# Opening of a decoder-layer kernel: memory keys' projection with all low parts on Vector, loads in halves, the identity loaded by itself, and the second memory block transposed behind the first products

## The chip, the cores and the metric

One core of a Trainium2 chip. The time is device microseconds of one launch, the median of three runs. A profile is taken of one further execution; its rows give microseconds from the start of the span.

## The reference

One inference step of one decoder layer, for a prompt of 512 rows and a sample group of 8 x 4 rows, width 1024: a mixer (mLSTM heads beside differential attention), cross-attention into 256 memory tokens, and a gated MLP with a causal convolution. The change lies in how the kernel opens: with the memory keys of the cross-attention.

```python
def mem_kv(mem, g_mem_src, w_mk, w_mv):
    B = mem.shape[0]
    mn = rms_norm(mem, g_mem_src)
    mk = (mn @ w_mk).reshape(B, MEM_TOKENS, MEM_HEADS, MEM_HEAD_DIM)
    mv = (mn @ w_mv).reshape(B, MEM_TOKENS, MEM_HEADS, MEM_HEAD_DIM)
    return mk, mv

def rms_norm(x, g):
    xf = x.astype(jnp.float32)
    y = xf * lax.rsqrt(jnp.mean(xf * xf, axis=-1, keepdims=True) + RMS_EPS)
    return (y * g.astype(jnp.float32)).astype(x.dtype)

# layer(): the mixer's input is projected next, and memory keys are used later
    h = rms_norm(x, g_mix_pre)
    z = h @ w_in
```

`mem` is 256 x 1024 and `w_mk` 1024 x 1024, all in float32; `mk` is also an output.

## The kernel before, in words

**Products in three.** Each float32 operand is split into a high part, cast to a rounded 32-bit format on ScalarE (`nc.scalar.copy`), and a low part, the difference, on Vector (`tensor_tensor` with SUB). A product a x b is high x high + high x low + low x high: three matmuls (L411, L412 and L413 in `gemmA`; L472 and L485 in `gemmB`). `split` writes both parts; `put` does it for activations and can give the low part to another engine, and `split_w` does it for weights.

**Memory keys.** `mem_k` computes two halves of 512 columns each. A half takes 8 steps of k (128 rows of the weights each) for two blocks of 128 memory rows: 2 x 8 x 2 x 3 = 96 matmuls of 128x128 by 128x512. A weight tile (`slotA`) holds two steps of k, 256 x 512 float32, 512 KB; eight of them, in a ring of 4 slots of split tiles behind 6 staging buffers. `W.get` takes the next tile, `W.free` gives a slot back, and `W.pump` then issues the next tile's load and split. With `share=True` a tile is cast whole on ScalarE (L221); Vector and GpSimd then compute one half of its low part each (L223).

**Memory rows.** `mem_in(b)` loads a block (`xms`, 512 KB). `norm_turn` transposes it on TensorE against the identity (L332, eight 128x128 transposes in two groups of four), multiplies by the gain on Vector (L334, out `ht`), and splits it by `put` into `memT` (L146 the high part, L147 the low part); with `pool=(True, False)` the first group's low part is GpSimd's, the second's Vector's. The root mean square isn't applied to the rows but to the result: `mrs` (sum of squares on ScalarE, L309; power on GpSimd, L304; copy on Vector, L540) scales the accumulator in `ev` (L548). The scaled result is stored and transposed for the cross-attention.

**The opening.** Block 0's rows, the constants `cpk` (identity, rotary tables and small selectors, 199 KB) and one row of gains are loaded. Nine warm-up matmuls run (`NWARM`), the gains are transposed (L177), block 0 is turned, seven fill matmuls follow (`NFILL`), and block 1 is turned. `W.nslots` is 1, then 2, then 4 between the loads, which sets in which order weight tiles and rows are asked for.

**The x blocks.** While `mem_k` runs, the prompt's rows (four blocks of 128, and 32 sample rows) are normalised and turned into `hT` at the steps of `mem_k` named by `HSTEPS`. A step is a yield of `gemmA`: steps 0 to 7 are the first half's k, 8 its end, 9 to 16 the second half's k, 17 its end. Behind `mem_k` the next projection (`gemmB`, L472) reads `hT`; it works through the first 256 columns of `hT` (two blocks) before it needs the others.

**Order.** Each engine and each DMA queue (SP's and ScalarE's) works in order. The order is made by a scheduler from the program's order as priority and its own idea of times; `tc.issue_after(ins)` puts what is traced in it behind `ins` on that engine, and `tc.high_priority()` (in `burst`) ahead of the rest.

## Time and profile before

| | |
|---|---|
| median of 3 runs | 939.5 us (939.25 to 940.07) |
| the profiled execution | 939.88 us, span 938.1 us |
| TensorE (PE) busy | 914.0 us, 97% of the span, 6778 matmuls |
| Vector (DVE) busy | 607.4 us, 65% |
| ScalarE (ACT) busy | 377.8 us, 40% |
| GpSimd (POOL) busy | 223.7 us, 24% |
| DMA | 130.59 MB, mean 139 GB/s |
| mean granted TensorE clock | 0.996 |

A row of a timeline gives start, duration, engine, line, operation, output<-inputs, shape and count; in brackets at its end stands the engine's idle time before it and what ended that. "ACTq" and "SPq" rows are DMA issues on the queues of ScalarE and SP. A row with xN covers N instructions one after the other. TensorE is busy in nearly all of the span, so what matters is where it isn't.

### The profile page before, as it was taken

The page shows a single profiled execution, that of the slowest core. Times are in us where ns is not written, and L with a number is a line of the kernel's source. Part 1 is how long each engine was busy: PE and PEld are TensorE (multiplying, and loading weights), DVE is VectorE, ACT ScalarE, POOL GpSimd, SP SyncE. Part 2 cuts the span into 40 slices and gives each one's busy share as a digit, 9 for nine tenths or more (in the row PEclk, how much of TensorE's full clock was granted, in tenths as well). Part 3 has the DMA queues.
Part 4 walks back from the last instruction along what each step waited for, and adds up shares of the span by engine and source line. Part 5 has one row for each costly group of instructions (what it writes and reads, how often), then busy time and mean ns, then how long its engine had stood idle before and what let it go on. Part 6 is the DMA issues. An engine that isn't in the chain of part 4 may idle for free.

```text
span 938.1 us, 17455 instructions
## 1 busy us (share of the span) xinstructions
PE 914.0 (97%) x6778; PEld 798.0 (85%) x6778; DVE 607.4 (65%) x1130; ACT 377.8 (40%) x728; POOL 223.7 (24%) x474
## 2 busy tenths in 40 slices
PE   7999999999999999999999999999999999999994
PEld 5899787879866778998777899889988998999974
DVE  5845144565887438686645778637757775776767
ACT  5745233344586447724434533322212222222232
POOL 6611000034442116570000553001100110110114
PEclk9999999999999999999999999999999999999998
DMA  8950023334780339967956632062054304413023
GB/s 286 311 180 11 1 90 138 90 103 161 243 296 8 136 117 298 310 201 243 312 189 172 198 115 69 26 180 69 27 135 135 92 5 120 128 48 90 24 94 117
DMA packets 120834, 130.59 MB, mean 139 GB/s; under 512 B 8599, under 2 KB 86264, under 8 KB 120752
## 3 DMA queue, kind: packets, MB, share of 16 engines
q1 hardware_dynamic: 114568, 125.96, 42.8%
q10 hardware_dynamic: 6184, 3.53, 1.3%
q8 instruction: 53, 0.87, 0.4%
q14 instruction: 29, 0.24, 0.1%
HBM read 112.54 MB, written 16.93 MB: 138 GB/s over the span
## 4 chain that ended last, share of the span: by engine, by line
PE 79%; DVE 8%; DMA 5%; ACT 3%; issue 3%; POOL 2%; SPq 0%; DVEq 0%; ACTq 0%; POOLq 0%
PE mm L485 31%; PE mm L411 6%; PE mm L412 6%; PE mm L413 6%; PE mm L472 4%; PE mm L1837 3%; PE mm L1841 3%; PE mm L1840 3%; PE sda L1256 2%; DVE xb L1165 2%; DMA wst<-in_cache_mem_k_dram 1%; PE mm L390 1%; PE cpo L1480 1%; DVE wslot L147 1%; PE oda L1284 1%
## 5 line engine op out<-in xcount | busy, mean ns | idle before, releaser
L485 PE MATMUL mm<-fT,wslot 128*128 128x256 f32 x1872 | 235.9, 288 | 0.0
L485 PEld LDWEIGHTS mm<-fT,wslot 128*128 128x128 f32 x1872 | 234.3, 188 | 1.8 <-issue 0.8
L146 ACT CAST wslot<-wst 128x1024 fp32r<-128x1024 f32 x125 | 130.7, 1050 | 261.0 <-issue 72.5
L147 DVE TENSOR_TENSOR wslot<-wst,wslot 128x1024 fp32r<-128x1024 f32 x125 | 154.3, 1238 | 81.7 <-ACT wslot L146 81.1
L1837 PE MATMUL mm<-wslot,act 128*128 128x512 f32 (+1 forms) x180 | 69.3, 387 | 0.0
L1840 PE MATMUL mm<-wslot,act 128*128 128x512 f32 (+1 forms) x172 | 67.0, 391 | 0.0
L1841 PE MATMUL mm<-wslot,act 128*128 128x512 f32 (+1 forms) x172 | 66.8, 392 | 0.0
L1739 POOL COPY cvo<-u 128x2 f32<-128x2 f32 x43 | 10.4, 243 | 217.1 <-DVE u L1737 217.1
L411 PE MATMUL mm<-wslot,hT 128*128 128x512 f32 x128 | 51.3, 402 | 0.0
L413 PE MATMUL mm<-wslot,hT 128*128 128x512 f32 x128 | 51.0, 399 | 0.0
L485 PE MATMUL mm<-hT,wslot 128*128 128x256 f32 (+1 forms) x384 | 50.9, 289 | 0.0
L412 PE MATMUL mm<-wslot,hT 128*128 128x512 f32 x128 | 50.8, 397 | 0.0
L1734 DVE TENSOR_TENSOR u<-mm,rsb 128x256 f32<-128x256 f32 x43 | 18.1, 423 | 48.9 <-PE mm L485 48.8
L485 PEld LDWEIGHTS mm<-hT,wslot 128*128 128x128 f32 x384 | 49.2, 188 | 0.5 <-issue 0.2
L1837 PEld LDWEIGHTS mm<-wslot,act 128*128 128x128 f32 x180 | 34.3, 191 | 8.0 <-issue 0.4
L1841 PEld LDWEIGHTS mm<-wslot,act 128*128 128x128 f32 x172 | 32.3, 188 | 6.9 <-issue 0.4
L1840 PEld LDWEIGHTS mm<-wslot,act 128*128 128x128 f32 x172 | 32.3, 188 | 6.9
L1751 ACT ACTIVATE c<-c 128x560 f32<-128x560 f32 x21 | 14.1, 672 | 56.8 <-DVE c L1745 56.7
L1745 DVE SCALAR_TENSOR_TENSOR c<-u,cvT,c 128x560 f32<-128x560 f32 x43 | 34.3, 798 | 0.9
L1744 DVE SCALAR_TENSOR_TENSOR c<-u,cvT,c 128x560 f32<-128x560 f32 x43 | 34.1, 793 | 0.2
L1852 DVE TENSOR_TENSOR yp<-mm,yp 128x512 f32<-128x512 f32 (+1 forms) x41 | 27.1, 672 | 5.1 <-PE mm L1841 5.1
L413 PEld LDWEIGHTS mm<-wslot,hT 128*128 128x128 f32 x128 | 24.1, 188 | 5.0
(493 smaller groups left out, 1858.0 us busy)
## 6 DMA issues: line engine op xcount, KB each, us to landing
wst<-in_w_up_dram SPq DMA_DIRECT2D x42, 512.0 KB
wst<-in_w_in_dram SPq DMA_DIRECT2D x28, 512.0 KB
wst<-in_w_down_dram SPq DMA_DIRECT2D x20, 512.0 KB
kvt<-in_cache_mem_k_dram SPq DMA_DIRECT2D x10, 512.0 KB
kvt<-in_cache_mem_v_dram SPq DMA_DIRECT2D x10, 512.0 KB
wst<-in_w_mk_dram SPq DMA_DIRECT2D x8, 512.0 KB
xb<-in_x_prompt_dram SPq DMA_DIRECT2D x8, 512.0 KB
wst<-in_cache_dk_dram SPq DMA_DIRECT2D x16, 256.0 KB
```

The source lines that it names most:

```text
L146: nc.scalar.copy(out=hi, in_=src)
L147: (eng or nc.vector).tensor_tensor(out=lo, in0=src, in1=f32(hi), op=SUB)
L411: mm(ps[b], lhsT=xt.hi(k, c0, c0 + n), rhs=s[:, 0, kk, :], start=(k == 0), stop=False)
L412: mm(ps[b], lhsT=xt.hi(k, c0, c0 + n), rhs=s[:, 1, kk, :], start=False, stop=False)
L413: return mm(ps[b], lhsT=xt.lo(k, c0, c0 + n), rhs=s[:, 0, kk, :], start=False, stop=(k == nk - 1))
L472: done[0] = mm(ps, lhsT=s[:, l, k, :], rhs=x(k, c0, c1), start=(k == 0 and l == 0 and x == xt.hi), stop=(k == 7 and x == xt.lo))
L485: mm(ps[i], lhsT=s[:, l, k, :], rhs=x(k, c0, c1), start=(k == 0 and j == 0), stop=(k == 7 and j == 2))
L1744: STT(out=c, in0=u[:, 1:EXT - 1], scalar=w[1], in1=c, op0=MUL, op1=ADD)
L1745: STT(out=c, in0=u[:, 0:EXT - 2], scalar=w[0], in1=c, op0=MUL, op1=ADD)
L1837: mm(ps, lhsT=t[:, 0, c0:c0 + P], rhs=s[:, 0, i % 2, cs], start=st, stop=False)
L1840: mm(ps, lhsT=t[:, 0, c0:c0 + P], rhs=s[:, 1, i % 2, cs], start=False, stop=False)
L1841: return mm(ps, lhsT=t[:, 1, c0:c0 + P], rhs=s[:, 0, i % 2, cs], start=False, stop=en)
```

## The change

- The identity has a tile of its own (64 KB), loaded first on ScalarE's queue; the gain row follows it there, off SP's queue. The other constants are loaded on SP's queue behind the second weight tile.
- The memory rows are loaded in two halves of 512 columns. The first two weight tiles of the first half of `mem_k` are loaded, cast and split in two halves each (one step of k each).
- All low parts of the memory keys' weights, of `memT` and of `hT` are on Vector.
- `gemmA` has `first`: products of block 1 at k = 0 and 1 are held; block 1 is turned behind block 0's first three products, and the held ones follow. Products of k > 1 are issued behind the transposes last traced at that point.
- `HSTEPS` goes from (1, 4, 7, 10, 13) to (5, 7, 9, 11, 13); the second x block is loaded at step 1, the other gains are transposed at step 5, and the sums of squares of the memory rows are made at step 3 with their copies on GpSimd.

```diff
-    HORD, HSTEPS = [0, 1, 2, 3, 4], (1, 4, 7, 10, 13)
+    HORD, HSTEPS = [0, 1, 2, 3, 4], (5, 7, 9, 11, 13)
...
-    cpk = cst.tile([P, MASK0], F32, name="cpk")
+    ident = cst.tile([P, P], F32, name="ident")
+    cpk = cst.tile([P, MASK0 - P], F32, name="cpk")
...
     def mem_in(b):
-        dma(out=xms[b], in_=I["mem_prompt"][0, b * P:(b + 1) * P, :])
+        for c in (slice(0, 512), slice(512, DM)):
+            dma(out=xms[b][:, c], in_=I["mem_prompt"][0, b * P:(b + 1) * P, c])
 
     mem_in(0)
-    nc.scalar.dma_start(out=cpk, in_=I["consts"][:, :MASK0])
-    grow = gains_in(0, 1, nc.sync)
+    nc.scalar.dma_start(out=ident, in_=I["consts"][:, :P])
+    grow = gains_in(0, 1, nc.scalar)
...
     def split_w(sv, st, share):
 
-        if share != True:
-            split(sv[:, 0], sv[:, 1], st, share or None)
+        if share:
+            for k in range(2):
+                split(sv[:, 0, k], sv[:, 1, k], st[:, k])
             return
-        m = st.shape[1] // 2
-        nc.scalar.copy(out=sv[:, 0], in_=st)
-        for e, c in ((nc.vector, slice(0, m)), (nc.gpsimd, slice(m, 2 * m))):
-            e.tensor_tensor(out=sv[:, 1, c], in0=st[:, c], in1=f32(sv[:, 0, c]), op=SUB)
+        split(sv[:, 0], sv[:, 1], st)
...
             if nrow == 256:
-                dma(out=st, in_=w[r0:r0 + 256, n0:n0 + 512].rearrange("(k p) n -> p k n", p=P))
+                for k in range(2) if share else ():
+                    dma(out=st[:, k], in_=w[r0 + k * P:r0 + k * P + P, n0:n0 + 512])
+                if not share:
+                    dma(out=st, in_=w[r0:r0 + 256, n0:n0 + 512].rearrange("(k p) n -> p k n", p=P))
                 split_w(sv, st, share)
...
     def norm_T(x, n, gname, xt, c0):
-        norm_turn(norm_rows(x, n), n, gname, xt, c0)
+        norm_turn(norm_rows(x, n), n, gname, xt, c0, (False, False))
...
                 for b in blocks:
-                    if b < 4:
-                        t = one(b, k, s)
+                    if first and b and k < 2:
+                        held.append((b, k, s))
+                    elif b < 4:
+                        with tc.issue_after(turned[0].ins) if first and k > 1 else nullcontext():
+                            t = one(b, k, s)
+                if first and k == 0:
+                    ahead = t.ins
+                if first and k == 1:
+                    with tc.issue_after(ahead):
+                        first()
+                    for x in held:
+                        t = one(*x)
...
     for n0 in (0, 512):
-        slotsA(w_mk, n0, True)
+        for k in range(0, 8, 2):
+            slotA(w_mk, k, n0, share=(n0 == 0 and k < 4))
...
     mem_in(1)
     W.nslots = 2
     W.pump()
+    dma(out=cpk, in_=I["consts"][:, P:MASK0])
     kept = []
-    for b in range(2):
-        kept.append(norm_turn(xms[b], P, "g_mem_src", memT, b * P))
-        if b == 0:
-
-            t = turned[0].ins
-            fill = mmp("fill")
-            for _ in range(NFILL):
-                with burst(t):
-                    t = mm(fill, lhsT=warm[:, 0:P], rhs=warm, start=True, stop=True).ins
-    for b in range(2):
-        VCP(out=mrs[:, b:b + 1], in_=rstd(sumsq(xms[b], P, N("hN")), P, 1, DM))
+
+    def turn(b):
+        kept.append(norm_turn(xms[b], P, "g_mem_src", memT, b * P, (False, False)))
+
+    turn(0)
+    t = turned[0].ins
+    fill = mmp("fill")
+    for _ in range(NFILL):
+        with burst(t):
+            t = mm(fill, lhsT=warm[:, 0:P], rhs=warm, start=True, stop=True).ins
...
-            yield from gemmA(memT, 8, [0, 1], ev)
+            yield from gemmA(memT, 8, [0, 1], ev, first=None if i else lambda: turn(1))
...
-    gains(1, 5, gains_in(1, 5, GQ))
-    VTS(out=gT[:, 36:40], in0=gT[:, 36:40], scalar1=1.0 - LAM_INIT, scalar2=None, op0=MUL)
-    h_in(HB[1])
+    grow = gains_in(1, 5, GQ)
     for i, _ in enumerate(mem_k()):
+        if i == 1:
+            h_in(HB[1])
+        if i == HSTEPS[0]:
+            gains(1, 5, grow)
+            VTS(out=gT[:, 36:40], in0=gT[:, 36:40], scalar1=1.0 - LAM_INIT, scalar2=None, op0=MUL)
+        if i == 3:
+            for b in range(2):
+                nc.gpsimd.tensor_copy(out=mrs[:, b:b + 1], in_=rstd(sumsq(xms[b], P, N("hN")), P, 1, DM))
         if i in HSTEPS:
             j = HSTEPS.index(i)
             norm_T(xbs[HB[j]], rows(HB[j])[1], "g_mix_pre", hT, rows(HB[j])[0])
```

## The prediction

> **What bounds the kernel now.** I read the page first, then busy time in stretches, then the TensorE timeline of the first 40 us, the chain of waits, and the other engines' and the DMA issuing queues' timelines for the same stretch.

> ```profile
> span 938.1 us, 17455 instructions
> ```
> ```profile
> 0.00:15.00 15.00, 10.29 (x43) 5.46 (x44) 6.44 (x13) 9.00 (x14) 8.47 (x18) 1.00 0.90 291
> 15.00:66.00 51.00, 51.00 (x342) 46.79 (x343) 33.62 (x45) 30.37 (x51) 26.42 (x31) 1.00 0.83 256
> 66.00:340.00 274.00, 270.85 (x1968) 221.60 (x1967) 152.72 (x368) 127.98 (x298) 56.63 (x76) 1.00 0.36 116
> ```
> After the stretch's length these rows give busy time of PE, PEld, DVE, ACT and POOL, then granted clock, DMA share and GB/s. TensorE has no hole from 15 to 66 us and 3.15 us of them in the 274 us behind. What the change touches can therefore only pay before 15 us, and pays in full only if nothing runs dry between 15 and 66 us.

> ```profile
> 5.59 0.19 PE L177 MATMUL gps<-cpk,grow 8*128 8x8 f32 x1 [0.34 <-DMA grow<-in_g_mem_src_dram]
> 5.71 1.09 PE L332 MATMUL tp<-cpk,xm 128*128 128x128 f32 x8
> 6.64 1.67 PE L538 MATMUL fill<-warm 128*128 128x512 bf16 x7
> 9.08 0.50 PE L411 MATMUL mm<-wslot,memT 128*128 128x512 f32 x1 [0.77 <-ACT memT L146]
> 9.42 1.03 PE L332 MATMUL tp<-cpk,xm 128*128 128x128 f32 x8
> 12.10 0.50 PE L413 MATMUL mm<-wslot,memT 128*128 128x512 f32 x1 [1.41 <-POOL memT L147]
> ...
> 14.83 0.50 PE L412 MATMUL mm<-wslot,memT 128*128 128x512 f32 x1 [0.87 <-DVE wslot L223]
> ```
> ```profile
> L411 PE MATMUL mm<-wslot,memT x32: 387/389/497, 9.1 to 36.3; 128*128 128x512 f32 x32
> ```
> ```profile
> 36.96 1.45 PE L472 MATMUL mm<-hT,wslot 128*128 128x256 f32 x11
> ```
> L411, L412 and L413 have 32 matmuls each: 96 in the memory keys' projection. Before 14.83 us only 9 of them and the 16 transposes of both memory blocks are done. From 14.83 to 36.96 us come the other 87 matmuls, 20 transposes at about 0.11 us (the pace of the eight at 9.42, whose 1.03 us hold the full length of the last one), and one gain transpose of about 0.2 us; (22.13 - 20 x 0.11 - 0.2) / 87 = 0.227 us is one matmul's pitch. 9 matmuls are worth 2.0 us, so the stall in the opening, counted from the end of the fill at 8.31 us, is 14.83 - 8.31 - 2.0 - 1.0 (the second block's transposes) = 3.5 us.

> What ends last there:

> ```profile
> 1.63 5.82 DMA wst<-in_w_mk_dram
> ```
> ```profile
> 7.47 1.04 ACT L221 CAST wslot<-wst 128x1024 fp32r<-128x1024 f32 x1 [1.06 <-DMA wst<-in_w_mk_dram]
> 8.42 0.61 ACT L146 CAST memT<-ht 128x512 fp32r<-128x512 f32 x1
> ```
> ```profile
> 8.59 1.78 POOL L223 TENSOR_TENSOR wslot<-wst,wslot 128x512 fp32r<-128x512 f32 x1 [1.45 <-ACT wslot L221]
> 10.33 1.72 POOL L147 TENSOR_TENSOR memT<-ht,memT 128x512 fp32r<-128x512 f32 x1
> ...
> 12.93 1.29 POOL L223 TENSOR_TENSOR wslot<-wst,wslot 128x512 fp32r<-128x512 f32 x1
> ```
> ```profile
> 8.54 0.69 DVE L223 TENSOR_TENSOR wslot<-wst,wslot 128x512 fp32r<-128x512 f32 x1 [0.62 <-ACT wslot L221]
> 10.21 0.71 DVE L147 TENSOR_TENSOR memT<-ht,memT 128x512 fp32r<-128x512 f32 x1 [0.97 <-ACT memT L146]
> 10.84 1.28 DVE L334 TENSOR_TENSOR ht<-tp,gT 128x512 f32<-128x512 f32 x2
> ...
> 13.08 1.70 DVE L223 TENSOR_TENSOR wslot<-wst,wslot 128x512 fp32r<-128x512 f32 x1
> ```
> ```profile
> 34.59 1.21 DVE L147 TENSOR_TENSOR wslot<-wst,wslot 128x1024 fp32r<-128x1024 f32 x1
> ```
> The first weight tile lands at 7.45 us; ScalarE casts it whole, ahead of memT; then GpSimd's halves of the low parts follow each other, 1.78 and 1.72 us, and the third product (the memory's low part) waits until 12.10. The same half tile takes Vector 0.69 us, but 1.70 us where GpSimd works on one beside it (13.08). A whole tile on Vector takes 1.21 us.

> **The change part by part.**

> *Loads.* Sizes and issue costs:

> ```profile
> cpk<-in_consts_dram ACTq DMA_DIRECT2D x1, 199.0 KB
> wst<-in_w_mk_dram SPq DMA_DIRECT2D x8, 512.0 KB
> ```
> ```profile
> 0.75 0.40 SPq L183 DMA_DIRECT2D xm<-in_mem_prompt_dram  x1
> 1.21 0.37 SPq L167 DMA_DIRECT2D grow<-in_g_mem_src_dram  x1
> ```
> ```profile
> SPq L231 <- DMA cpk<-in_consts_dram: 2.7, 1, 2.7
> ```
> ```profile
> 5.00:10.00 5.00, 3.89 (x24) 2.49 (x24) 2.47 (x6) 3.36 (x6) 2.46 (x4) 1.00 1.04 334
> ```
> Ahead of the first usable piece of weights stood 512 (rows) + 199 + 4 + 512 = 1227 KB; now 512 + 64 (the identity, 128 x 128 x 4 B) + 4 + 256 = 836 KB. 391 KB less at 334 GB/s is 1.2 us: the half tile lands near 6.25 us. The second half comes 0.8 us behind, at about 7.05. Five issues are added to SP's queue (rows +2, tiles +2, the rest of the constants) and one is taken from it (the gain row, now on ACT's queue behind the identity): net four at 0.40 = 1.6 us. They lie beside transfers that fill the 16 engines (share 1.04), so they cost nothing; without that cover it is 1.6 us. SP also waits for earlier transfers before it issues (2.7 us for the constants' landing at 5.26); the identity lands sooner than they did, so this wait shrinks. The rest of the constants (135 KB, 0.4 us of bandwidth) goes ahead of the third weight tile, whose need comes later (below); its first reader in the trace is far off:

> ```profile
> 59.79 0.22 DVE L1293 SCALAR_TENSOR_TENSOR cv<-cpk,nlam 128x1 f32<-128x1 f32 x1 [5.91 <-POOL nlam L634]
> ```

> [...]

> *Rows and transposes of block 0.* TensorE is in order and its nine warm-up matmuls, unchanged, run on:

> ```profile
> 1.32 3.92 PE L193 MATMUL warm<-warm 128*128 128x512 bf16 x9 [1.32 <-POOL mhalf L196]
> ```
> They end at 5.24 us, so the gain transpose moves from 5.59 to 5.25 at best: 0.35 us. Fill now ends near 8.0. First product possible at about 8.1 instead of 9.08.

> *Low parts all on Vector.* To finish the first two weight tiles and both memory blocks Vector has four scalings, four memory low parts and four half-tile low parts: 12 x 0.64 (1.28/2) = 7.7 us from about 6.1, so 13.8; the third tile's 1.21 brings 15.0. GpSimd's three rows above did 1.78 + 1.72 + 1.29 of it beside Vector, at the price of Vector's 1.70; that cover is gone, and Vector carries its work in the 7.7.

> *Second block turned later.* Block 0's six products of k = 0 and 1 (1.4 us) go ahead of block 1's eight transposes (1.0 us), block 1's own six follow. Nothing is added to TensorE, only order: 24 products and 8 transposes need 24 x 0.227 + 1.0 = 6.4 us from 8.1, that is 14.5 us; Vector makes it 15.0. Against before, TensorE at 15.0 has 24 products behind it rather than 9: 15 x 0.227 = 3.4 us, less 15.0 - 14.83 = 0.2. **Gain of the opening: 3.2 us.**

> *Sums of squares of the memory rows to step 3, copies on GpSimd.*

> ```profile
> 5.05 1.06 ACT L309 ACTIVATE hN<-xm 128x1024 f32<-128x1024 f32 x1 [2.37 <-DMA xm<-in_mem_prompt_dram]
> ```
> Two at 1.06 us on ScalarE, first used when the first half's results are scaled, 24 products after 15.0 at about 20 us; hidden. Without that cover ScalarE would scale 2.1 us late, and TensorE only meets that when it runs out of accumulators (five banks, two a half).

> *Steps of the x blocks from 1, 4, 7, 10, 13 to 5, 7, 9, 11, 13; gains at step 5; second x load at step 1.* Here is a wait that is added. Products of k > 1 of the first half are issued behind the transposes last traced, and from k = 6 these are x block 0's. Behind them on TensorE's queue are 12 products of k = 6 and 7. Block 0's rows are loaded behind the weight tiles on SP's queue:

> ```profile
> 11.07 0.34 SPq L585 DMA_DIRECT2D xb<-in_x_prompt_dram  x1
> ...
> 18.49 1.46 SPq L231 DMA_DIRECT2D wst<-in_w_mk_dram  x3
> ```
> ```profile
> 17.06 0.37 ACTq L600 DMA_DIRECT2D mem_d<-ht  x1
> 17.46 2.00 ACT L221 CAST wslot<-wst 128x1024 fp32r<-128x1024 f32 x2 [3.31 <-DMA grow<-in_g_ffn_pre_dram]
> ```
> ScalarE stood 3.31 us because a store on its queue waited for a small gain row to land; the fourth tile's cast came only at 17.46. That was free. With TensorE dense from 15.0 with 24 products done, k = 6 is wanted at 15.0 + 12 x 0.227 = 17.7 us. If the cast stays at 17.46, that tile's low part is ready at 17.46 + 1.05 + 1.21 = 19.7: a stall of 2.0 us. If the store falls behind the cast in ScalarE's order, it is 0. x block 0's transposes can leave a hole at this same point, if its rows land late; the two overlap and don't add, and products of the second half can be put in between. I take 0.9, between 0 and 2.0: both ends hang on an order that the trace of before doesn't show, and no row is nearer to one.

> *Sum.* 3.2 - 0.9 = 2.3 us. The profiled execution took 939.88 us (938.1 of span, 1.8 around it), 0.38 above the median of 939.5. 939.88 - 2.3 = 937.6 for that execution, **937.2** against the median. The saving should travel: from 15 us TensorE sets the pace and later waits hang on what it frees.

> **The rivals.**

> *A later supply takes most of it (937.6 to 939.7).* Besides the fourth tile, the last three memory-key tiles were issued at 18.49 us, and their casts are:

> ```profile
> 24.19 1.05 ACT L221 CAST wslot<-wst 128x1024 fp32r<-128x1024 f32 x1
> 25.50 1.05 ACT L221 CAST wslot<-wst 128x1024 fp32r<-128x1024 f32 x1 [0.25 <-DMA wst<-in_w_mk_dram]
> ```
> The new pace wants the sixth tile (60 products done) at 15.0 + 36 x 0.227 = 23.2 us; unchanged, it is whole at 24.19 + 1.05 + 1.21 = 26.4. Then 3.2 us are lost and nothing remains: 939.5. For it: added issues sit ahead of these. Against it: the tiles are asked for as slots come free, and these come free earlier.

> *Nothing runs dry (935.4 to 936.3).* The full 3.2, and 0.3 to 0.9 more if scaling and low parts interleave better than my Vector sum: 939.5 - 3.2 = 936.3 and below.

> *Slower: the second x block isn't ready when its projection starts.*

> ```profile
> 36.44 0.62 ACT L146 CAST hT<-ht 128x512 fp32r<-128x512 f32 x1 [0.86 <-DVE ht L334]
> ```
> This high part ended at 37.06, against 36.96 + 8 x 0.117 = 37.9 us at which the ninth product of the next projection needs it. Its step moves from 4 to 7: three steps of six products, 4.1 us. If it slides in full it ends at 41.2 while TensorE comes to that point at 37.9 - 3.2 = 34.7: a stall of 6.5 us, 3.3 us slower than before, 942.8. The point of decision is an end of 37.9 us: behind it the kernel is slower. Against it: with its step at 4 (about 19 us) it ran 17 us late, held by loads and Vector, not by the step.

> *TensorE's clock falls back.* Warm-up matmuls ran at 3.92/9 = 0.44 us, the fill's at 1.67/7 = 0.24: the array starts at about half speed. A long hole after the fill could bring that back: about 3.9 us at half speed, a loss near 1.9 us: 939.1. Before, with holes of 1.41 us at most, the granted clock stayed 1.00. [...]

> **How the numbers follow.** Forecast (936.3 to 937.6) 0.38; nothing dry 0.17; later supply 0.33; clock 0.04; slower 0.08. What a measurement can tell from no change is 0.2%, 1.9 us: 937.6 to 941.4. Faster is 0.38 + 0.17 = 0.55, same 0.33 + 0.04 = 0.37, slower 0.08. The range 935.8 to 939.8 leaves out the last third of the second case (0.06) and the slower case with a little of the third (0.1).

> **What would show it.** Right: first product near 8.1 us, 24 products done by 15.0, no low part of a memory tile on GpSimd, Vector's halves all near 0.65 us, the next projection (L472 of before) starting near 34.7 us instead of 36.96. The 0.9: a hole of TensorE at 17 to 20 us behind ScalarE's cast or x block 0's transposes. Wrong: the next projection at 36 us or later, holes with a weight tile's DMA as releaser between 20 and 30 us, or the gain present at 40 us and gone at 350.

## The result: slower, with the opening's gain lost again before 29 us

| | before | changed |
|---|---|---|
| median, same chip | 939.24 us (937.76 to 940.07) | 942.78 us (941.28 to 945.44, 8 runs) |
| ratio | | 1.004, 95% interval 1.0025 to 1.0055 |
| the profiled execution | 939.88 us, span 938.1 | 942.74 us, span 941.0 |
| mean granted TensorE clock there | 0.996 | 0.994 |

The forecast was 937.2 us with a range of 935.8 to 939.8. The change made the kernel 3.5 us slower.

The same three stretches of the changed kernel's profile as were shown of before (length, then busy time of PE, PEld, DVE, ACT and POOL, granted clock, DMA share, GB/s):

```profile
0.00:15.00 15.00, 12.25 (x51) 6.80 (x52) 7.37 (x14) 6.11 (x10) 1.47 (x10) 1.00 0.80 242
15.00:66.00 51.00, 46.57 (x298) 41.68 (x297) 30.75 (x49) 32.33 (x54) 9.08 (x25) 0.97 0.85 258
66.00:340.00 274.00, 270.85 (x1983) 222.67 (x1983) 154.17 (x369) 128.29 (x298) 56.20 (x76) 1.00 0.37 118
```

TensorE works 2.0 us longer before 15 us (12.25 against 10.29): the gain that was meant. From 15 to 66 us it works 4.4 us less (46.57 against 51.00), where it had not stood still at all before, and its clock is 0.97. From 66 to 340 us its busy time is the same to 0.01 us: nothing new happens there, the loss only travels. The next projection, for which the prediction named 34.7 us if it was right and 36 us or later if it was wrong, started at 43.44 us (36.96 before). The first long row of 32 matmuls by `wst` is a convenient landmark (before, then changed):

```profile
117.01 1.93 PE L390 MATMUL mm<-wst,xts 128*32 128x256 f32 x32
```
```profile
121.94 1.93 PE L392 MATMUL mm<-wst,xts 128*32 128x256 f32 x32
```

It comes 4.9 us later. (2.0 us of this are given back later, behind 435 us; the spans differ by 2.9.) TensorE's timeline of the changed kernel shows where the 4.9 us arise:

```profile
8.60 0.50 PE L413 MATMUL mm<-wslot,memT 128*128 128x512 f32 x1 [0.76 <-ACT memT L146]
9.75 0.50 PE L415 MATMUL mm<-wslot,memT 128*128 128x512 f32 x1 [0.41 <-DVE memT L147]
...
16.30 0.39 PE L415 MATMUL mm<-wslot,memT 128*128 128x512 f32 x1
18.45 0.73 PE L413 MATMUL mm<-wslot,memT 128*128 128x512 f32 x2 [1.76 <-ACT wslot L146]
19.71 0.50 PE L414 MATMUL mm<-wslot,memT 128*128 128x512 f32 x1 [0.53 <-DVE wslot L147]
...
22.20 0.24 PE L177 MATMUL gps<-ident,grow 32*128 32x32 f32 x1
24.58 0.79 PE L413 MATMUL mm<-wslot,memT 128*128 128x512 f32 x2 [2.14 <-ACT wslot L146]
```

The first product comes at 8.60 us instead of 9.08 and the third at 9.75 instead of 12.10. Then TensorE stands still for 1.76, 0.53 and 2.14 us, and behind that its clock falls. In windows of 2 us (PE busy, granted clock, DMA share, GB/s):

```profile
22.00:24.00 2.00, 0.44 (x3) 1.00 0.97 359
24.00:26.00 2.00, 1.42 (x6) 0.78 1.02 388
26.00:28.00 2.00, 2.00 (x9) 0.50 1.08 370
28.00:30.00 2.00, 2.00 (x9) 0.87 1.19 299
```

A clock of 0.78, 0.50 and 0.87 over three windows is 0.44 + 1.00 + 0.26 = 1.7 us lost. Together: 2.0 gained, 4.4 lost standing still, 1.7 lost to the clock make 4.1 of the 4.9 us; the rest is not assigned.

Who was late? The DMA queue of SP, the beginning of the chain of waits, and ScalarE with its queue, all of the changed kernel:

```profile
5.95 0.96 SPq L231 DMA_DIRECT2D wst<-in_w_mk_dram  x2
8.17 0.33 SPq L542 DMA_DIRECT2D cpk<-in_consts_dram  x1
9.34 1.27 SPq L233 DMA_DIRECT2D wst<-in_w_mk_dram  x2
18.26 0.40 SPq L233 DMA_DIRECT2D wst<-in_w_mk_dram  x1
```
```profile
6.33 3.89 DMA bif<-in_b_if_dram
10.22 0.02 issue
10.24 0.38 SPq L233
10.62 0.04 issue
10.66 7.58 DMA xb<-in_x_prompt_dram
18.24 0.02 issue
18.26 5.15 DMA wst<-in_w_mk_dram
```
```profile
15.38 0.62 ACT L146 CAST memT<-ht 128x512 fp32r<-128x512 f32 x1 [2.03 <-DMA mem_d<-ht]
16.94 0.37 ACTq L619 DMA_DIRECT2D mem_d<-ht  x1
17.35 2.00 ACT L146 CAST wslot<-wst 128x1024 fp32r<-128x1024 f32 x2 [1.35 <-DMA mem_d<-ht]
```

Before, SP issued weight tiles 2 to 5 in one run that ended at 9.31 us:

```profile
5.26 4.05 SPq L231 DMA_DIRECT2D wst<-in_w_mk_dram  x4
```

Now the third and fourth go out at 9.34 and 10.24. The chain shows what SP waited for: the fourth tile's issue at 10.24 stands behind the landing of `bif` (four numbers, 3.89 us on their way, issued on the other queue), and the fifth tile's issue at 18.26 behind the landing of x block 0 at 18.24. Some of the waits of SP's queue in the first 30 us (engine and line, what ended the wait, us, times, longest) name more of the kind:

```profile
SPq L170 <- DMA wst<-in_w_mk_dram: 2.5, 1, 2.5
SPq L184 <- DMA ident<-in_consts_dram: 2.2, 1, 2.2
SPq L542 <- DMA xm<-in_mem_prompt_dram: 1.2, 1, 1.2
SPq L169 <- DMA wst<-in_w_mk_dram: 0.9, 1, 0.9
SPq L233 <- DMA xb<-in_x_prompt_dram: 0.9, 1, 0.9
SPq L233 <- DMA bif<-in_b_if_dram: 0.5, 1, 0.5
```

The last gain rows (L169, L170) have nothing to do with weight tiles, and still they wait until one has landed. Between x block 0's issue and the fifth tile's stand seven others on the two queues (five gain rows, two stores `mem_d`): here an issue waits for the eighth one before it, whatever its size. The records of the trace say why. The kernel's 377 loads and stores (372 before) report their landing on only eight semaphores, the counters by which one engine waits for another, and an issue waits until the last transfer with its own semaphore has landed. That order of eight is the program's over both queues; in the order in which the issues start it is six to ten back in the first 27 us. So the eight are the program's semaphores. I call them *places*.

The first stand, of 1.76 us, comes behind 24 products, so it is the third tile that is missing. Its load had landed by 14.34 us, when the gain row that waited for it (L169) went out, but its cast started at 17.35: two stores ahead of it on ScalarE's queue waited for their places, 2.03 and 1.35 us. The third stand ends with the fifth tile, whose products are put ahead of those of k = 6 and 7, since these are tied behind x block 0's transposes (25.4 us). The DMA engines had less to do meanwhile, as the first 12 us show (before, then changed):

```profile
0.00:12.00 12.00, 8.26 (x35) 1.00 0.86 273
```
```profile
0.00:12.00 12.00, 9.44 (x41) 1.00 0.74 223
```

273 x 12 = 3.3 MB before, 223 x 12 = 2.7 MB after.

### The profile page after: what moved, and what is told of

Same layout as the page of the kernel before. It is cut to its first block, busy times and chain, and to the rows that moved or that the text cites. A ratio compares the mean times of both kernels' runs of the same rounds, so it can differ in the third digit from the quotient of the medians.

```text
span 941.0 us, 17459 instructions
## 1 busy us (share of the span) xinstructions
PE 915.8 (97%) x6778; PEld 799.1 (85%) x6778; DVE 607.1 (65%) x1137; ACT 378.5 (40%) x730; POOL 199.1 (21%) x461
## 4 chain that ended last, share of the span: by engine, by line
PE 86%; DVE 6%; DMA 4%; ACT 2%; issue 1%; POOL 0%; SPq 0%; DVEq 0%; ACTq 0%; POOLq 0%
PE mm L497 32%; PE mm L413 7%; PE mm L414 7%; PE mm L415 7%; PE mm L484 6%; PE mm L1856 3%; PE mm L1860 3%; PE mm L1859 3%; PE sda L1275 2%; PE mm L392 1%; PE cpo L1499 1%; DVE wslot L147 1%; DMA wst<-in_w_mk_dram 1%; PE oda L1303 1%; PE tp L334 1%
## 5 line engine op out<-in xcount | busy, mean ns | idle before, releaser
L146 ACT CAST wslot<-wst 128x1024 fp32r<-128x1024 f32 (+1 forms) x135 | 139.4, 1037 | 265.7 <-issue 76.4
L147 DVE TENSOR_TENSOR wslot<-wst,wslot 128x1024 fp32r<-128x1024 f32 (+1 forms) x135 | 164.3, 1220 | 85.0 <-ACT wslot L146 84.5
L413 PE MATMUL mm<-wslot,hT 128*128 128x512 f32 x128 | 51.3, 402 | 0.0
L413 PE MATMUL mm<-wslot,memT 128*128 128x512 f32 x64 | 25.3, 410 | 4.8 <-ACT wslot L146 3.9
## 6 DMA issues: line engine op xcount, KB each, us to landing
wst<-in_w_up_dram SPq DMA_DIRECT2D x42, 512.0 KB
wst<-in_w_in_dram SPq DMA_DIRECT2D x28, 512.0 KB
wst<-in_w_down_dram SPq DMA_DIRECT2D x20, 512.0 KB
kvt<-in_cache_mem_k_dram SPq DMA_DIRECT2D x10, 512.0 KB
kvt<-in_cache_mem_v_dram SPq DMA_DIRECT2D x10, 512.0 KB
xb<-in_x_prompt_dram SPq DMA_DIRECT2D x8, 512.0 KB
wst<-in_w_out_dram SPq DMA_DIRECT2D x8, 512.0 KB
```

The source lines that it names most:

```text
L146: nc.scalar.copy(out=hi, in_=src)
L147: (eng or nc.vector).tensor_tensor(out=lo, in0=src, in1=f32(hi), op=SUB)
L413: mm(ps[b], lhsT=xt.hi(k, c0, c0 + n), rhs=s[:, 0, kk, :], start=(k == 0), stop=False)
```

## The experiments

Theory S (supply): the halves add loads, these take places, the bytes come later, TensorE stands still. Theory C (clock): a long stand costs again as much by a fallen clock. The rivals: Vector is the new bound; or one particular wait (the third and fourth tile behind ScalarE's stores, the fifth behind x block 0, the order of products) is the loss and can be mended alone. In the expectations up to b1 the late supply is also called theory A, the order of products theory B, and Vector as the bound rival C. "Landmark" is the row shown above, by its start in the chain of waits, 0.07 us behind that of the row. The time is a median with the ratio to the kernel before on the same chip. "Traced" is the time of the profiled execution, from which the columns to its left come. In e1, e10, e11, c1, e13 and e14 it is the fastest of all, by up to 5.6 us below the median, so their traces can't show what the slower executions paid for. Stands are those of the first 60 us, and later ones with a fall behind them; a fall at the very end (930 to 937 us), which every trace has, is left out.

| run | MB by 12 us | landmark, us | longest stands, us (at) | falls of the clock at, us | traced, us | median, us | ratio (95%) |
|---|---|---|---|---|---|---|---|
| before | 3.3 | 117.1 | 1.4 (10.7) | none | 939.88 | 939.24 to 939.73 | |
| changed | 2.7 | 122.0 | 2.1 (22.4) | 25.1 | 942.74 | 942.78 | 1.004 (1.0025 to 1.0055) |
| e1_tile4_early | 2.8 | 119.4 | 1.9 (43.5) | none | 941.11 | 946.71 | 1.0079 (1.0064 to 1.0094) |
| e2_stores_late | 2.7 | 122.6 | 2.3 (12.5), 2.3 (40.8) | 15.6, 42.9 | 943.40 | 943.4 | 1.0053 (1.0034 to 1.0071) |
| e3_untied | 2.8 | 119.4 | 2.3 (16.1), 1.9 (436.5) | 19.1, 438.9 | 943.15 | 943.34 | 1.0051 (1.0032 to 1.0071) |
| e4_all_three | 2.6 | 122.6 | 2.1 (12.8), 2.4 (43.7) | 15.1, 45.8 | 945.66 | 945.63 | 1.0064 (1.0042 to 1.0086) |
| e5_small_late | 3.4 | 119.1 | 2.5 (19.4) | 470.7 | 942.53 | 942.07 | 1.0025 (1.001 to 1.0039) |
| e6_whole_loads | 3.3 | 117.8 | 0.6 (20.6) | none | 939.67 | 940.21 | 1.0006 (0.9996 to 1.0016) |
| e7_gpsimd_back | 2.7 | 123.3 | 1.5, 4.3 (19.2, 20.9) | 23.3 | 944.95 | 945.35 | 1.0069 (1.0048 to 1.009) |
| b1_lows_on_vector | 3.4 | 116.4 | 0.9 (10.8) | none | 938.91 | 940.58 | 1.002 (0.9999 to 1.0042) |
| b2_halves_on_before | 2.7 | | | | | 942.02 | 1.0024 (1.0011 to 1.0038) |
| b2_again | 2.8 | 118.6 | 1.3 (10.8) | none | 941.95 | one run | |
| e10_whole_small_early | 3.6 | 118.8 | 1.2 (40.5) | none | 940.58 | 943.55 | 1.0043 (1.0026 to 1.006) |
| e10_again | 3.6 | 119.1 | 1.6 (40.6) | none | 940.97 | one run | |
| e11_whole_nohold | 3.3 | 117.6 | 0.9 (44.6) | none | 939.95 | 942.23 | 1.0022 (1.001 to 1.0034) |
| c1_keep_warm | 2.8 | 121.6 | 2.7 (16.4) | 20.6 | 942.18 | 944.58 | 1.0047 (1.003 to 1.0063) |
| e13_rows_whole | 3.2 | 119.7 | 2.3 (20.1) | none | 941.21 | 943.78 | 1.0045 (1.0031 to 1.0059) |
| e14_weights_whole | 3.1 | 120.3 | 1.5 (21.2) | none | 942.50 | 943.86 | 1.0059 (1.0036 to 1.0083) |
| e5b_small_late_untied | 3.4 | 123.0 | 4.1 (39.2) | 42.2 | 945.64 | 945.15 | 1.0059 (1.0042 to 1.0076) |
| a2_changed_again | 2.9 | 121.7 | 3.5 (16.1), 2.0 (438.1) | 20.8, 440.7 | 945.12 | one run | |

The traced execution of b2_halves_on_before ran at a mean granted clock of 0.752 (1128.23 us), so its landmark isn't given; b2_again supplies it. On the chip of b2_again and e10_again the kernel before took 940.92 us, in its one run there.

**One late supply mended at a time** (e1 to e4). The fifth weight tile asked for ahead of x block 0; the stores behind the first scaled keys, with the gain rows' transpose held in place; the tie of k = 6 and 7 to x block 0's transposes taken away; all three.

```diff
e1 +    pre[4] = v2(stage(), 512)
e1 +    dma(out=pre[4], in_=w_mk[0:256, 512:1024].rearrange("(k p) n -> p k n", p=P))
e2 +            with tc.issue_after(scaled1[0]):
e2                  nc.scalar.dma_start(out=mem_d[:, 4 * q:4 * q + 4, b * P:b * P + P], in_=t)
e3 -    with tc.issue_after(turned[0].ins) if first and k > 1 else nullcontext():
e3 +    with tc.issue_after(tied) if first and k > 1 else nullcontext():   # block 1's transposes
```

> The changed kernel, and one load moved: the fifth memory-key weight tile is loaded ahead of the first x block and the six small gain rows on SP's queue (in the changed kernel it is issued at 18.26 us, behind them). Theory A, late supply: the hole of TensorE at 22.4 to 24.6 us, whose releaser is that tile's cast, goes, and with it the fall of the granted clock behind it (0.50 at 26 to 28 us): 2.1 + 1.6 us less, near 939.1 us. Theory B, the order: the last 12 products of the first half stay behind x block 0's transposes, which wait for its rows; the hole is only partly filled, 940 to 942. Rival C, Vector is the bound with all the low parts: no change, 942.8.

> The changed kernel, and the four stores of the turned memory rows are issued on ScalarE's queue behind the first half's scaling instead of in between the casts (the gain transpose is kept behind step 5's products, where the changed kernel has it). Theory A: casts no longer stand 2.0 and 1.4 us behind the stores, the hole at 16.7 to 18.5 us goes, but the fifth tile still lands at 23.4 us and the next hole grows by as much: 942 to 943.5, no gain alone. If the stores alone were the cause: 1.8 us less and no clock fall, near 939.5. Rival C: 942.8, with the hole still there and Vector as its releaser.

> The changed kernel, and the products of k > 1 are issued behind the second memory block's transposes alone, no longer behind x block 0's from k = 6 on. Theory B: 12 products (2.7 us) fill the hole at 22.4 to 24.6 us, the clock doesn't fall, 2.1 + 1.6 us less: near 939.1. Theory A alone: the products run, but the hole comes back behind them when the fifth tile isn't there: 940 to 942. Rival C: 942.8.

> The three edits together: fifth tile early, stores late, products not behind x block 0's transposes. Theories A and B: the holes between 16 and 25 us (4.4 us) and the clock fall (1.6 us) go: 942.8 - 6.0 = 936.8, faster than before. Rival C, Vector the bound: not below 940.

None came near the time before. e1 and e4 were slower than any time expected of them (rival C gave only a floor for e4), and e3's time is that of no change, though its landmark came 2.6 us earlier. e2's median lies in the range of theory A (942 to 943.5), but its next stand came at 40.8 us and not at the fifth tile. Each stand that was mended turned up elsewhere. The rows of the longest stands in e2, e3 and e1:

```profile
14.83 1.15 PE L415 MATMUL mm<-wslot,memT 128*128 128x512 f32 x2 [2.29 <-ACT wslot L146]
43.13 1.11 PE L336 MATMUL tp<-ident,hN 128*128 128x128 f32 x4 [2.33 <-ACT mkT L572]
```
```profile
18.40 0.73 PE L413 MATMUL mm<-wslot,memT 128*128 128x512 f32 x2 [2.28 <-ACT wslot L146]
```
```profile
45.45 1.09 PE L339 MATMUL tp<-ident,hN 128*128 128x128 f32 x8 [1.94 <-ACT mkT L574]
```

The fifth tile early or the tie gone brings the landmark from 122.0 to 119.4 us (2.6 us), but the timed runs don't follow: e1's traced execution took 941.11 us, its six others 946.0 to 948.6. Mending any one of these waits did not bring the time back.

**What feeds the waits** (e5, e6, e7, b1). In the changed kernel: page table, `wg`, `b_if` and `m0` behind the first scaled keys on ScalarE's queue; both halved loads whole again; half of the low parts back on GpSimd. In the kernel before: all low parts on Vector and nothing else.

```diff
e5 +    with tc.issue_after(scaled1[0]):
e5          SQ.dma_start(out=wg, ...)          # and ptab, bif, m0
e6 -        for c in (slice(0, 512), slice(512, DM)):
e6 -            dma(out=xms[b][:, c], in_=I["mem_prompt"][0, b * P:(b + 1) * P, c])
e6 +        dma(out=xms[b], in_=I["mem_prompt"][0, b * P:(b + 1) * P, :])
e6 -                for k in range(2) if share else ():      # weight tiles likewise
e7 +        for e, k in ((nc.vector, 0), (nc.gpsimd, 1)):
e7 +            e.tensor_tensor(out=sv[:, 1, k], in0=st[:, k], in1=f32(sv[:, 0, k]), op=SUB)
b1 -        slotsA(w_mk, n0, True)
b1 +        slotsA(w_mk, n0)                   # and (False, False) in norm_turn, norm_T
```

> The changed kernel with five small loads (page table, gate weights, two bias rows, a state row), which ScalarE's queue issues in the first 8 us, issued behind the first half's scaling. Theory S, transfers in flight: a transfer waits for the eighth one before it, so halved loads and small loads take places that hold few bytes, and the 16 engines run dry (243 GB/s at 6 to 8 us and 190 at 10 to 12, where before had 338 and 362). Then the third and fourth weight tile are issued near 7 us, not 9.3, 10 to 12 us is full, and the landmark (the first group of 32 matmuls that the chain shows, 117.08 us before and 122.01 after) comes 1 to 3 us earlier. Rival C, Vector is the bound: landmark near 122.

> The changed kernel with the memory rows and the first two weight tiles loaded whole again (split and cast still in halves). Theory S: four transfers fewer, the third and fourth tile are issued before 8 us, 6 to 12 us carry above 300 GB/s; the first product comes 0.8 to 1.2 us later, but the holes at 16 to 25 us shrink: landmark near 119 to 121, between before and after. If the halves only helped: later than 122.01 by about 1.

> The changed kernel with the low parts divided between Vector and GpSimd as before. Rival C, Vector is the bound with all of them: the landmark comes 1 us or more earlier than 122.01. Theories A and S: no gain, and a loss of up to 2 us where GpSimd's 1.7 us parts stand in the opening: 122 to 124.

> The kernel before with this one part of the change: all low parts of the memory keys' weights, of memT and of hT on Vector. Theories A and S: the wait of 1.4 us for GpSimd's memory part goes and nothing is added to the queues: landmark 115 to 116.5, 1 to 2 us faster than before. Rival C: the same or slower than before, 117 to 119.

e6 is the clearest run: with the loads whole and all other parts of the change left in, the landmark goes from 122.0 back to 117.8, the median from 942.8 to 940.2, and the difference to before is no longer measurable. It went better than expected (landmark 119 to 121). One part of the expectation failed: the first product was to come 0.8 to 1.2 us later, and came at 8.45 us, 0.15 us earlier than in the changed kernel. There too it waits for the cast of `memT`; the half weight tile, whose cast started at 5.95 us instead of e6's 6.74, was not what it waited for. The first 12 us and the landmark of e6:

```profile
0.00:12.00 12.00, 9.83 (x40) 1.00 0.87 279
```
```profile
117.74 1.93 PE L389 MATMUL mm<-wst,xts 128*32 128x256 f32 x32
```

e5 keeps the halves and takes the small loads off the places: the bytes come back in full (282 x 12 = 3.4 MB), though the tie to x block 0 leaves a stand of 2.5 us. So the places, not the size of the pieces, held the bytes up. But the bytes alone don't decide the time: e5 (3.4 MB) is still 2.6 us slower than before on its chip, and e5b and e10 below, with 3.4 and 3.6 MB, 5.5 and 3.8 us. That Vector is the bound is refuted from both sides: giving GpSimd its share back is slower still (landmark 123.3), and all low parts on Vector in the kernel before bring the landmark forward to 116.4, though its time isn't better than before.

**The halves alone, the rest without them, and the clock** (b2, e10, e11, c1). b2 is the kernel before with both halved loads. e10 is e6 with e1's, e3's and e5's edits. e11 is e6 with block 1 turned right behind the fill. c1 is the changed kernel with eight products of zeros behind the gain rows' transpose.

```diff
b2 +            dma(out=xms[b][:, c], in_=I["mem_prompt"][0, b * P:(b + 1) * P, c])      # two c
b2 +                    dma(out=st[:, k], in_=w[r0 + k * P:r0 + k * P + P, n0:n0 + 512])  # two k, first two tiles
e11 -            yield from gemmA(memT, 8, [0, 1], ev, first=None if i else lambda: turn(1))
e11 +            yield from gemmA(memT, 8, [0, 1], ev)     # turn(1) ahead of mem_k
c1 +        for _ in range(8):
c1 +            with burst(t.ins):
c1 +                t = mm(gps[:, n:n + 384], lhsT=warm[:, 0:P], rhs=warm[:, :384], start=True, stop=True)
```

> The kernel before with one part of the change alone: the memory rows and the first two weight tiles are loaded in halves (four more loads, the same bytes). Theory S (places of the queue: a load waits for the eighth one before it, so four more small loads push the next weight tiles' issues back): 2.5 to 2.9 MB moved in the first 12 us (3.27 before, 2.64 in the changed kernel), wst loads 3 and 4 issued behind 8 us, the 1.86-us weight-load landmark at 119 to 121.5 us (117.08 before), time 941 to 943. Rival (the halves only bring the first products forward; the late supply comes from the other parts): landmark at 116 to 117.5, MB as before, time 938.5 to 940.

> The changed kernel with whole loads again, and besides: the fifth weight tile's load issued ahead of x block 0 and the gain rows, products of k=6,7 not tied behind x block 0's transposes, the small loads on ScalarE's queue (page table, wg, b_if, m0) behind the first scaled keys. Theory S: the opening has neither the holes at 20.2 and 21.3 us (0.80 and 0.58) of the version with whole loads alone nor places held by small loads; landmark at 115 to 117, time 937 to 939.2, granted clock 0.996 or more. Rival (a late supply mended only moves the hole, as in the four earlier versions): landmark at 117.5 to 120, time 940 to 943.

> The changed kernel with whole loads, and the second memory block turned right behind the fill instead of behind the first block's products. Theory S (loads decide, the order of the turn is nearly free): landmark within 0.8 of the version with whole loads alone (117.8), so 117.0 to 118.6, time 939.5 to 941. Rival (as the prediction had it, the held turn brings 8 products forward, 1.8 us): landmark at 119.2 to 120, time 941.5 to 942.5.

> The changed kernel with the transpose of the gain rows put right behind a product and eight 384-column products of zeros behind it, into a part of its tile that nobody reads: TensorE works on where it stood still for 2.1 us at 22.4 to 24.6 us. Theory C (the fall of the clock to 0.50 at 26 to 28 us comes from that idle stretch and costs about 1.6 us): PEclk 0.95 or more at 24 to 30 us, landmark at 120.0 to 121.0 (122.0 in the changed kernel), time 941.0 to 942. Rival (the clock falls for another reason, or the products that follow wait for their tile anyway): landmark at 121.7 to 122.8, time 942.5 to 944.

b2 is the other half of e6's proof: the halves alone make the kernel before 1.0024 times slower (942.02 us), as theory S had it. What they add to before (2.3 us) and what taking them away saves in the changed kernel (942.78 - 940.21 = 2.6 us, or 2.8 us with each kernel measured against before on its own chip) agree within the noise. e10 missed: TensorE is fed better than ever in the first 12 us (3.6 MB), yet the landmark is 118.8, with a stand of 1.2 us at 40.5 us that ends with the copy of the transposed keys, and the median 943.55. e11's landmark fits theory S (117.6), its time the rival (942.23): turning block 1 later is worth nothing that the trace shows, and 2 us in the timed runs; these don't agree, and this stays open.

In c1 the dummies did what they were for at 24 us, and yet the kernel was not faster, since in that run the longest stand came earlier, at the third tile:

```profile
19.07 0.73 PE L417 MATMUL mm<-wslot,memT 128*128 128x512 f32 x2 [2.65 <-ACT wslot L146]
```
```profile
20.00:22.00 2.00, 1.67 (x4) 0.64 0.92 268
22.00:24.00 2.00, 2.00 (x6) 0.51 1.04 408
24.00:26.00 2.00, 2.00 (x12) 1.00 1.05 406
```

At 24 to 26 us the clock is 1.00, where the changed kernel had 0.78; at 20 to 24 us it is 0.64 and 0.51, where that had 1.00. In these two runs the fall goes with idle time, not with a place in the program. The time, 944.58, is worse than even the rival's (942.5 to 944).

**Which half, and how the loss differs from run to run** (e13, e14, e5b, a2, b2_again, e10_again). e13 has the rows whole, e14 the weight tiles; e5b has both halves, e5's and e3's edits. The last three are second traces of the changed kernel, of b2 and of e10.

> The changed kernel with the memory rows loaded whole again (two loads fewer), the weight tiles still in halves. Theory S (each load more holds a place): about half of the way back: MB by 12 us between 2.8 and 3.1 (2.64 changed, 3.29 with both whole), landmark 118.5 to 121, time 940.5 to 942.5, with a clock fall only where an idle stretch of over 2.2 us is left. Rival (only the weight halves matter): MB 2.6 to 2.75, landmark 121.5 to 122.5, time 942.5 to 943.5.

> The changed kernel with the first two weight tiles loaded whole again (two loads fewer), the memory rows still in halves. Theory S: as for the rows, MB 2.8 to 3.1, landmark 118.5 to 121, time 940.5 to 942.5. Rival (only the weight halves matter): MB 3.2 or more, landmark 117.5 to 118.5, time 939.7 to 940.7.

> The changed kernel with both halves kept, the small loads on ScalarE's queue behind the first scaled keys and the products of k=6,7 not tied behind x block 0's transposes. Theory S (the halves cost by the places alone): MB by 12 us 3.2 to 3.5, the hole of 2.67 us at 19.05 of the version with the small loads late gone or under 1.3, landmark 116.5 to 118.5, time 939.5 to 941.5. Rival (a late tile takes the tie's place): a hole of 1.5 us or more between 15 and 25 us, landmark 118.5 to 121, time 941.5 to 943.5.

> The changed kernel once more, for a second trace. Theory C (an idle stretch of over 2.2 us of TensorE is followed by some 3.3 us at clock 0.50, worth 1.65 us): every fall in the first 60 us stands 3 to 4 us behind the start of such a stretch, and the run's time differs from 942.7 by about 1.7 us for each fall more or less. Rival (the falls come of their own): falls without such a stretch ahead, or stretches of over 2.4 us without a fall.

> The kernel before with the halved loads alone once more, for a trace at full clock. Theory S: MB by 12 us 2.6 to 2.9, landmark 118.5 to 121.5, time 940 to 943; where an idle stretch of over 2.2 us stands in the opening, a fall of the clock to 0.50 for some 3.3 us behind it. Rival (the halves alone do nothing in the opening): landmark 116.5 to 117.6.

> The version with whole loads, the fifth tile early, no tie and the small loads late once more, for a second trace. Theory C: if the run takes 943 us or more, its trace has one or two falls of the clock of 3 us that the first trace (940.6) has not, each behind an idle stretch of over 2.2 us; if it takes about 940.6 it has none. Rival (the loss is spread over the run): 943 or more and no fall, the landmark within 0.5 of 118.75 and the rest longer.

Neither half alone is to blame: each undone gives back about as much (landmark 119.7 and 120.3, 3.2 and 3.1 MB), and the two together 4.2 us. By the traced executions (941.21 and 942.50) they fit theory S, by the medians (943.8) not: in time, half of the halves undone gave nothing back, and this stays open. b2_again shows the halves alone at full clock: landmark 118.6, 1.6 us behind before, and its first tiles' issues:

```profile
6.16 1.63 SPq L234 DMA_DIRECT2D wst<-in_w_mk_dram  x2
7.83 0.97 SPq L236 DMA_DIRECT2D wst<-in_w_mk_dram  x2
```

The second tile's two halves go out from 6.16 to 7.79 us and the third tile at 7.83, where before issued the whole second tile at 5.26 and had the fifth out by 9.31. The mark of 8 us expected for the third is just missed; the delay is real and lies one tile earlier. e5b missed: with its bytes on time it stood 4.1 us at 39 us, and landmark and time (123.0, 945.15) are worse than the rival's:

```profile
43.35 1.09 PE L335 MATMUL tp<-ident,hN 128*128 128x128 f32 x4 [4.11 <-DVE hN L321]
```

There the transposes of a later x block wait for its rows to be normalised. e10_again took 940.97 us and had no fall, as theory C has it for a run near 940.6; so the slower runs of e10 have no trace, and why their median is 943.55 stays open.

a2 is the most telling trace. Besides a fall at 20.8 us, behind a stand of 3.5 us at the third tile, it has one at 440 us, far from the change, where the first trace's clock is 1.00:

```profile
438.00:440.00 2.00, 0.09 (x8) 1.00 0.70 215
440.00:442.00 2.00, 1.94 (x48) 0.67 0.66 224
442.00:444.00 2.00, 2.00 (x61) 0.50 0.41 52
```

In the nineteen traces at full clock TensorE stands there between two groups of products for 1.0 to 2.0 us. At 1.97 us (a2) and 1.87 us (e3) the clock fell; at 1.95 us (e1), and at 1.74 us and less in the others, it did not. So the length of a stand doesn't settle it; the last section says what goes with a fall. So a2 met its expectation in part: the first fall stands 4.7 us behind the start of its stand and not 3 to 4, the second behind a stand of less than 2.2 us. The fall costs 1.7 us; a2 took 2.4 us more than the first trace.

## Why the prediction was wrong

**The step that failed** is the one on loads: five issues added to SP's queue, "They lie beside transfers that fill the 16 engines (share 1.04), so they cost nothing", and SP's wait for earlier transfers, of which it said "this wait shrinks". Here the share was an outcome of the bytes asked for, not a cover. Each added issue takes one of eight places until it lands, and a load of a few bytes holds it too (3.89 us for `bif`, 5.15 us for the fifth weight tile's 512 KB). The wait grew: the third weight tile went out at 9.34 us, when before had issued the fifth, the share of the first 12 us fell from 0.86 to 0.74, and taking the halves away gave 2.6 to 2.8 us back. Nor did the halves buy what they were for: the cast of the half tile started at 5.95 us (landing forecast near 6.25), but the first product waits for `memT`, and with whole loads (e6) it came at 8.45 us against 8.60.

**The opening's gain, 3.2 us.** Its front held in part: the first product was forecast at about 8.1 and came at 8.60, and Vector's parts took 0.69 us each. But 24 products are done at 16.7 us, not by 15.0, half a microsecond of it from the late first product and most of the rest from short waits for `memT` (0.41 us at 9.75) and slower starts behind them. By 15 us TensorE had worked 2.0 us more than before, not 3.2. e6 shows that this step fails even without the halves: its opening has the early first product (8.45 us) and no gain at the landmark (117.8 against 117.1).

**The added wait, 0.9 us between 0 and 2.0.** Both mechanisms that the prediction named were at work, and its size was not right. ScalarE's stores did hold up a cast, but that of the third tile, which the sum had ready by 15.0: it started at 17.35, and 1.76 + 0.53 = 2.3 us were lost there, just over the upper end. The tie to x block 0's transposes left the stand at 22.4 us, which ended with the fifth tile; that one was not named there, is asked for behind x block 0 and the five gain rows, and came too late to fill it: another 2.1. "The two overlap and don't add" was wrong: they come one after the other.

**The rivals.** The later supply, given a chance of 0.33, is what happened, but its price was bounded by 3.2 us, as if a late tile could only take the gain back. It took 4.4. The fall of the clock had 0.04 and happened, for 1.7 us (3.41 us at 0.50). The prediction counted it as an alternative to late tiles; here it followed them, behind a stand of 2.14 us. The slower rival gave 942.8, the measured number, by a mechanism that did not happen: behind 30 us the changed kernel's TensorE waits for no `hT` before the next projection, and has no stand of over 0.1 us to 66 us. That agreement is chance.

**The sum over again.** Halves: 2.3 to 2.8 of the 3.5 us by which the median rose, shown by e6 and b2. The rest of the change together: 0.6 us by e6's ratio, not told from nothing. One reading of the prediction was off without effect: between 14.83 and 36.96 us lie 16 transposes and not 20, which makes the pitch 0.232 us. How much of the halves' price is standing and how much the clock differs from run to run.

## What to carry to other kernels

Count transfers, not only bytes: where an issue waits for the eighth one before it, as here, cutting a load in two, or a load of a few bytes ahead of a big one, can delay whatever comes eight issues later (the third weight tile went out at 9.34 us, where before had the fifth out by 9.31), and the DMA share shows it only afterwards. When a gain depends on TensorE running denser, list the next three supplies with the times at which they were asked for, since mending one only shows the next. Behind a stand of TensorE of about 2 us the clock fell in some executions, which cost 1.7 us more (1.97 us in a2), and not in others (1.95 us in e1), so read more than one trace before trusting a landmark.

## What the runs showed of the hardware

```profile
17.77:21.18 3.41, 2.34 (x11) 1.00 0.91 302
21.18:24.59 3.41, 1.91 (x12) 1.00 1.08 395
```
```profile
467.24:470.65 3.41, 1.61 (x79) 1.00 1.01 378
470.65:474.06 3.41, 3.41 (x37) 0.50 1.02 387
```

- At 1.54 us of work a window holds 3.41 - 1.54 = 1.87 us of idle time in all, and that was enough for a fall (438.9 us in e3). An estimate from these numbers: a stand of 2.1 us with full work around it is followed by a fall at (3.41 + 2.1 - 2 x 1.87) / 3.41, about half, of the grid's positions.
- So one kernel with a stand of about 2 us can take one fall more or fewer from execution to execution, as the changed one did. Wherever the grid might lie, between 7 and 920 us the trace of before has no window with less than 1.61 us of work and that of e6 neither; the changed kernel's first trace has one with 1.54 us or less at about nine of ten positions. Its eight timed runs lie accordingly: 941.28 us at a mean clock of 0.995, five at 942.7 to 942.9 (0.993 and 0.994; the traced one has one fall), two at 945.1 and 945.4 (0.991; a2, at 945.12, has two). A fall of 3.41 us at 0.50 is 0.0018 of the mean clock. Over 122 runs of the changed kernel and the fifteen others the time goes with the mean granted clock (correlation -0.78): 941.1 us on average above 0.9945 (49 runs), 945.3 up to 0.9925 (23 runs). Where the falls of the slower runs lay isn't known, since only the profiled ones have a trace; this also leaves open why e1, e10, e11, e13 and e14, whose traces have no fall, were 942 to 947 us in the median.
